# Two transfers of the norm's gain and bias: asked for earlier in layer A, as a repeating transfer into another buffer in layer B

## The chip, the cores and the metric

The kernel runs on one core of one Trainium2 chip. The metric is the device time of one launch in microseconds (us). Several executions are timed and their median is quoted; one more execution is profiled, and every start, duration and wait in this text is of that one.

## The reference

A decoder trunk of two layers over 256 tokens of width 1024, all float32. Layer A mixes the tokens with a gated linear recurrence (6 heads), layer B with stick-breaking attention (12 heads); both also attend to 256 memory tokens with 4 heads. Each layer ends in an output projection with a residual and a layer norm, and a mixture of 16 experts (2 per token) with a second residual and norm. What matters here, cut to its core:

```python
def post_norm(x, y, g, b):
    return layer_norm(DEEPNORM_ALPHA * x + y.astype(x.dtype), g, b)
...
        mixed = jnp.concatenate([seq_out.astype(x.dtype), mem_out.astype(x.dtype)], axis=-1)
        x = post_norm(x, mixed @ w_o[layer], ln_mix_g[layer], ln_mix_b[layer])
        moe_out = hier_moe(x, w_group[layer], b_group[layer], w_router[layer], b_router[layer],
                           w_gate[layer], w_up[layer], w_down[layer])
        x = post_norm(x, moe_out, ln_ffn_g[layer], ln_ffn_b[layer])
```

## The kernel before, in words

All weights are one array of 133 chunks, w0 to w132, each a tile of 128 partitions by 8 KB (1.05 MB). The class Stream sends them from SP's queue in the order of use. A chunk needs a free tile: from a ring of nine (tag w), or from a buffer that is idle just then and is lent to the stream by `stream.open(tags, end)` until chunk `end`. In the code no chunk is sent before the third one ahead of it has landed (DEPTH, L95 to L98), so at most three are in flight. A scheduler of the framework may exchange neighbours, but within an engine's queue the built order is fixed, and SP waits in that order.

The layer's second half is `mixer_end` (L937). For layer B (l = 1) it runs so. The last output projections give four sums of 128 tokens by 512. DVE adds the residual (L399, `Norm.add`). For the first half of the tokens ACT sums the squares (L406), DVE forms the variance (L409), POOL raises it to the power -0.5 (L410), and DVE continues with the shift (L413) and the ranking of that half's experts (`Moe.rank`, L580 to L597), in program order. Behind that stands the residual add of the last quarter of the tokens (L399 again), which PE needs for its transposes (L566), these for the second half's router logits (L573), then come the second half's statistics, its power (L424), ranking, slot counting (L604, L605) and the gather by a matrix of ones and zeros (L644). Then the experts begin: `Moe.run` works through eight pairs p = 0 to 7. Pair p of layer B uses chunks w85+6p to w90+6p: four for gate and up (L820; the first two in its first half, the next two in its second), two for down (L913). The first two products of pair p+1 are put between the gate and down products of pair p. w85 and w86 are sent on their own into tiles u and ex (L1574, L1575). Before the experts' end all engines read a count of tokens (`values_load`, L488); on SP that is one instruction, TENSOR_LOAD, that waits for a value from DVE, and chunks behind it wait with it.

The norm's gain and bias (two rows of 1024) must stand on all 128 partitions for the affine step (L438, L440: multiply and add, once for each half of the tokens). `rows` (L376) brings them into the tile gb: either ACT asks for 8 KB into one partition (L382) and POOL copies them to all partitions with two PARTITION_BROADCAST (L384), or, with `by_transfer`, one transfer writes the two rows to each of the 128 partitions (L380; 1.05 MB). Before, both layers' first norm use the former; the last norm of layer B uses the latter. POOL's broadcast belongs to a set of instructions of its own: the program loads it ahead (MODIFY_POOL_CONFIG at L384) and loads the other set back ahead of the next power (MODIFY_POOL_CONFIG at L410).

Around layer B's norm, buffers go to the stream like this: x0 and x1 (the projections' input, split in two) after the last projection (L1553); u, ex after the heads; m0, m1 and others in `mixer_end`; gb (which held the values vB until the last head product) only after the second affine step (L1078), until chunk 121.

Of the kernel before, what the change touches and what calls it, by code (L numbers as in the profile page):

```python
# [7 lines left out]
F32 = mybir.dt.float32  # L8
# [7 lines left out]
P = 128  # L16
D = 1024
T = 256
NT = 2
# [11 lines left out]
EXPERTS_END = (71, 133)  # L31
# [11 lines left out]
def trunk(ctx: ExitStack, tc: tile.TileContext, w_all, x_tok_d, cst_d, msk_d, rw_d, rb_d,  # L43
# [4 lines left out]
    slots = ctx.enter_context(tc.tile_pool(name="slots", bufs=1))  # L48
    keep = ctx.enter_context(tc.tile_pool(name="keep", bufs=1))
# [65 lines left out]
    def run(*gens):  # L115
        for g in gens:
            for _ in g:
                pass

    def chain(*gens):  # L120
        for g in gens:
            yield from g
# [10 lines left out]
    stream = Stream()  # L133
# [107 lines left out]
    def proj_feat(xs, evac, name, pre=None):  # L241

        w, i = pre[0] if pre else stream.get()
        xh, xl = xs
        ps = bank(f"{name}p", shape=(P, 2, T))
        for b in range(2):
            wh, wl = pre[1][b] if pre else split(w[:, b * HC:(b + 1) * HC], f"{name}{b}")
            for k in range(NK):
                s = slice(k * P, (k + 1) * P)
                nc.tensor.matmul(ps[:, b], wh[:, s], xh[:, k], start=(k == 0), stop=False)  # L250
                nc.tensor.matmul(ps[:, b], wh[:, s], xl[:, k], start=False, stop=False)
                nc.tensor.matmul(ps[:, b], wl[:, s], xh[:, k], start=False, stop=(k == NK - 1))
            if b == 0:
                yield
        stream.done(i)
        evac(ps)
        yield
# [8 lines left out]
    def proj_tok(xs, width, evac, name):  # L266

        c0 = 0
        while c0 < width:
            n = 512 if width - c0 >= 512 else 256  # L270
            kc = HC // n
            ps = [bank(f"{name}p{c0}_{t}", shape=(P, n)) for t in range(NT)]
            for k0 in range(0, NK, kc):
                hf = k0 // kc % 2
                if hf == 0:
                    w, i = stream.get()
                wh, wl = split(w[:, hf * HC:(hf + 1) * HC], f"{name}{c0}_{k0}")
                for k in range(kc):
                    for t in range(NT):
                        tok_mm(ps[t], xs, t, k0 + k, wh[:, k * n:(k + 1) * n], wl[:, k * n:(k + 1) * n],  # L280
                               k0 + k == NK - 1)
                if hf == 1:
                    stream.done(i)
                if k0 + kc < NK:
                    yield
            for t in range(NT):
                evac(t, c0, n, ps[t])
            yield
            c0 += n
# [22 lines left out]
    def mem_v(ms, l):  # L312
        return proj_tok(ms, 256, lambda t, c0, n, ps: nc.scalar.activation(memv[:, t], ps, AF.Copy), f"mv{l}")
# [59 lines left out]
    def tok_tile(which, name):  # L373
        return keep.tile([P, NT, D], F32, tag=which, name=name)

    def rows(which, name, by_transfer=False):  # L376

        gb = tok_tile("gb", f"gb{name}")
        if by_transfer:
            nc.scalar.dma_start(gb, ln_d[0, 2 * which:2 * which + 2].partition_broadcast(P))  # L380
            return gb
        nc.scalar.dma_start(gb[0:1], ln_d[:, 2 * which:2 * which + 2])  # L382
        for v in range(2):
            ins = nc.gpsimd.partition_broadcast(gb[:, v], gb[0:1, v])  # L384
            if which % 2:
                tc.keep_in_program_order(ins)
        return gb
# [44 lines left out]
    def affine(dst, z, gb, norms=None, ts=range(NT)):  # L432

        for t in ts:
            if norms:
                ins = nc.vector.scalar_tensor_tensor(dst[:, t], z[:, t], norms[t].r, gb[:, 0], op0=ALU.mult, op1=ALU.mult)
            else:
                ins = nc.vector.tensor_mul(dst[:, t], z[:, t], gb[:, 0])  # L438
            tc.keep_in_program_order(ins)
            tc.keep_in_program_order(nc.vector.tensor_add(dst[:, t], dst[:, t], gb[:, 1]))  # L440
# [493 lines left out]
            self.y = y  # L934


    def mixer_end(op, res, l, lasts, fill, finish):  # L937

        tags[0] = "m"
        s = res  # L940
        end = EXPERTS_END[l]
# [8 lines left out]
        norms = [Norm(f"x{l}{t}") for t in range(NT)]  # L950
# [117 lines left out]
        moe.start(work)  # L1068
        moe.indices()
        xg = moe.first_rows()  # L1070
        gb = rows(2 * l, f"m{l}")
        for p in moe.run(xg):
            if p == 0:
                x1 = moe.x1 = tok_tile("u", f"x1{l}")
                affine(x1, s, gb, ts=(0,))
            if p is None:
                affine(x1, s, gb, ts=(1,))
                stream.open(("gb",), end - 12, keep)  # L1078
            if p == 6 + l:
                gb = rows(2 * l + 1, f"o{l}", l == 1)  # L1080
        tags[0] = "my"
        z2 = tok_tile("v", f"z{l}")
        norms = [Norm(f"m{l}{t}") for t in range(NT)]
# [30 lines left out]
    with tc.tile_pool(name="lev", bufs=1) as lev:  # L1114
        q, kk, f = [slots.tile([P, NK, T], F32, tag=tag, name=name)[:, 0:NH]
                    for tag, name in (("o0", "q"), ("o1", "kk"), ("wc", "f"))]
# [125 lines left out]
        def ev_v(t, c0, n, ps):  # L1242
# [3 lines left out]
        fl = chain(proj_tok(xs, 768, ev_v, "ai"),  # L1246
                   proj_feat(xs, lambda ps: nc.scalar.activation(qm, ps, AF.Copy), "aqm"),
                   mem_k(ms, 0, load_split), mem_v(ms, 0))
# [7 lines left out]
    with tc.tile_pool(name="atta", bufs=1, reuse_waits="tile") as pool:  # L1256
        fl = proj_tok(xs, 768, ev_g, "ag")
# [14 lines left out]
    op = OutProj(mixed, 0, gn)  # L1272
    tags[0] = "m"
    op.start()
    with tc.tile_pool(name="hatt", bufs=1, reuse_waits="tile") as ha:
        def head(hg, t):
            po = bank("ho", shape=(P, 2, P))
            for j in range(2):
                h = 2 * hg + j
                hv = slice(h * P, (h + 1) * P)  # L1280
                if t == 0:
                    nc.tensor.matmul(po[:, j], AT[:, h, 0], v[:, 0, hv], start=True, stop=True)
                else:
                    nc.tensor.matmul(po[:, j], ATx[h // 3][:, h % 3], v[:, 0, hv], start=True, stop=False)
                    nc.tensor.matmul(po[:, j], AT[:, h, 1], v[:, 1, hv], start=False, stop=True)
            sq = ha.tile([P, 2, P], F32, tag="sq", name="sq", bufs=2)
            nc.scalar.activation(sq, po, AF.Square)  # L1287
            rms = ha.tile([P, 2], F32, tag="rms", name="rms", bufs=2)
            nc.vector.reduce_sum(rms, sq, axis=AX.X)
            nc.vector.tensor_scalar(rms, rms, 1.0 / P, RMS_EPS, op0=ALU.mult, op1=ALU.add)  # L1290
            nc.gpsimd.tensor_tensor(rms, rms, neghalf.to_broadcast([P, 2]), op=ALU.pow)  # L1291
            on = ha.tile([P, 2, P], F32, tag="on", name="on", bufs=2)
            nc.vector.tensor_mul(on, po, rms[:, :, None].to_broadcast([P, 2, P]))
            nc.vector.tensor_mul(on, on, gate[:, t].rearrange("p (h e) -> p h e", e=P)[:, 2 * hg:2 * hg + 2])
            return on

        def head_mixed(hg, t, on):
            pt = bank("hot", shape=(P, 2, P))
            for j in range(2):
                nc.tensor.transpose(pt[:, j], on[:, j], ident)  # L1300
            ks, ts_ = slice(2 * hg, 2 * hg + 2), slice(t * P, (t + 1) * P)
            nc.scalar.activation(mixed[0][:, ks, ts_], pt, AF.Copy)
            nc.vector.tensor_sub(mixed[1][:, ks, ts_], pt, mixed[0][:, ks, ts_])

        def heads():
            prev = None
            for hg in range(3):
                for t in range(NT):
                    on = head(hg, t)
                    if prev:  # L1310
                        head_mixed(*prev)
                    prev = hg, t, on
                    yield
            head_mixed(*prev)
            yield
        fl = op.main(range(3))
        weave(heads(), fl, 1)
        run(fl)
    x_tok = tok_tile("v", "x_tok")
    nc.scalar.dma_start(x_tok, x_tok_d)  # L1320
    stream.send(EXPERTS_END[0] - 48, keep, "u")
# [20 lines left out]
    fl = mem_v_fill()  # L1342
# [5 lines left out]
    def into_next(moe, work, add, norms, s, sc, gb):  # L1348
# [102 lines left out]
        stream.done(wk.chunk[1])  # L1451
        wparts.use(*free)
        wparts.turn = 2
    x2, gb, norms = mixer_end(op, x_tok, 0, [3], fl, into_next)


    mixed = fpair("o", "mixB")
    with tc.tile_pool(name="sbp", bufs=1, reuse_waits="tile") as sbp:
# [84 lines left out]
        fl = proj_tok(xs, 768, ev_v, "bv")  # L1543
        weave(sticks(range(4, 8)), chain(kq[2], qmp), 1.5)
        run(kq[2], qmp)
        with tc.tile_pool(name="attb", bufs=1, reuse_waits="tile") as pool:
# [3 lines left out]
            weave(chain(sticks(range(8, 12)), mem_attn(pool, qm, 1, prs, mixed, place)), fl, 6 / 14)  # L1550
            turned(11, betas.pop(11))
            run(fl)
    stream.open(("x0", "x1"), EXPERTS_END[1])  # L1553
    wparts.use("wa", "wb", "wc", "wd")
    op = OutProj(mixed, 1)
    tags[0] = "m"
# [13 lines left out]
    fl = op.main(range(2))  # L1570
    next(fl)
    weave(heads(), fl, 0.5)
    run(fl)
    stream.send(EXPERTS_END[1] - 48, keep, "u")  # L1574
    stream.send(EXPERTS_END[1] - 47, slots, "ex")  # L1575
    for q in (2, 3):
# [4 lines left out]
    def into_output(moe, work, add, norms, s, o, gb):  # L1581
# [10 lines left out]
        with tc.manual_schedule(engines={mybir.EngineType.DVE}):  # L1592
# [15 lines left out]
            gain(1, 1)  # L1608
            bias(1, 0)
            bias(1, 1)  # L1610
    mixer_end(op, x2, 1, [2, 3], iter(()), into_output)


# [88 lines left out]
```

## Time and profile before

| | us |
|---|---|
| median of 3 executions | 525.6 |
| lowest and highest | 524.14, 529.12 |
| the profiled execution's own time | 526.96 |
| its span (first to last instruction) | 525.3 |
| outside of the span | 1.66 |

PE is busy for 491.1 us of the span (93%), DVE for 300.2, ACT for 229.6, POOL for 62.9. The DMA engines moved 161.61 MB, 308 GB/s on average. The mean granted TensorE clock is 0.983.

The profile shows starts and durations on each engine, what ended the idle time before an instruction, and, by stretch, the share of the 16 DMA engines in use. An instruction that DMA issues is given without its landing; a landing shows indirectly, where the issue of a later chunk waits for it.

### The profile page before, as it was taken

The numbers are of one execution on the slowest core, as the hardware profiler recorded it, in microseconds if no ns is written. First come the engines' busy times: TensorE is split into PE (matmuls) and PEld (weight loads), VectorE is DVE, ScalarE is ACT, GpSimd is POOL, SyncE is SP. The second block draws the span as 40 slices with busy tenths as digits, with TensorE's granted clock in tenths as the row PEclk, the third lists the DMA queues.
The fourth block names the chain that finished last, engine by engine and source line by source line (L and its number), as shares of the span: only waits on it lengthen the run. The fifth ranks groups of instructions, "written<-read, shape, count | busy, mean of one in ns | idle before, by whom it ended". The sixth has DMA issues, their size and how long they took to land. (4 is left out here: it accounts for less than half of the span.)

```text
span 525.3 us, 9096 instructions
## 1 busy us (share of the span) xinstructions
PE 491.1 (93%) x3534; PEld 326.7 (62%) x3534; DVE 300.2 (57%) x682; ACT 229.6 (44%) x471; POOL 62.9 (12%) x78
## 2 busy tenths in 40 slices
PE   4999999999999999999797999998998899999992
PEld 4998898788996333333236889877687333333431
DVE  4668876867758622233338698677445842233547
ACT  4845446684445222333017566668423232222322
POOL 1100000002132111112011500000010121111201
PEclk9999999999999999999898999999998999999997
DMA  8999834447888999999999763242999799999922
GB/s 270 407 404 404 345 103 160 161 156 326 299 332 321 384 403 384 394 385 407 409 379 395 271 252 143 100 160 99 381 365 364 288 382 419 414 422 409 412 119 81
DMA packets 28439, 161.61 MB, mean 308 GB/s; under 512 B 5239, under 2 KB 5623, under 8 KB 11363
## 3 DMA queue, kind: packets, MB, share of 16 engines
q1 hardware_dynamic: 20736, 140.76, 68.3%
q0 software_dynamic: 4752, 10.94, 5.4%
q10 hardware_dynamic: 2902, 9.26, 4.8%
q8 instruction: 30, 0.49, 0.4%
q14 instruction: 19, 0.16, 0.1%
HBM read 158.92 MB, written 13.64 MB: 329 GB/s over the span
## 5 line engine op out<-in xcount | busy, mean ns | idle before, releaser
L820 PE MATMUL gu<-w,ex 128*64 128x512 f32 x256 | 62.9, 609 | 3.4 <-DMA w<-in_w_all_dram 2.3
L820 PE MATMUL gu<-w,xg 128*64 128x512 f32 x256 | 60.8, 601 | 0.1
L913 PE MATMUL po<-w,hT 128*64 128x512 f32 (+1 forms) x272 | 58.4, 570 | 0.1
L913 PEld LDWEIGHTS po<-w,hT 128*64 128x64 f32 x272 | 18.8, 136 | 34.0 <-issue 27.3
L820 PEld LDWEIGHTS gu<-w,ex 128*64 128x64 f32 x256 | 17.2, 137 | 34.8 <-issue 26.1
L820 PEld LDWEIGHTS gu<-w,xg 128*64 128x64 f32 x256 | 16.4, 136 | 26.5 <-issue 24.6
L920 DVE COPY hr<-po 128x512 f32<-128x512 f32 x10 | 6.9, 692 | 43.1 <-PE po L913 43.0
L629 ACT ACTIVATE xg<-xgp,lnT 128x128 f32<-128x128 f32 x32 | 13.5, 457 | 25.6 <-PE xgp L791 22.4
L918 DVE TENSOR_TENSOR hl<-po,hl 128x512 fp32r<-128x512 f32 (+1 forms) x14 | 8.5, 615 | 26.5 <-ACT hl L917 25.5
L627 DVE TENSOR_SCALAR xg<-xgp,lnT 128x128 f32<-128x128 f32 x32 | 12.4, 408 | 19.0 <-ACT xg L629 15.7
L629 ACT ACTIVATE ex<-xgp,lnT 128x128 f32<-128x128 f32 x32 | 14.3, 458 | 19.3 <-PE xgp L791 19.0
L627 DVE TENSOR_SCALAR ex<-xgp,lnT 128x128 f32<-128x128 f32 x32 | 13.1, 410 | 15.1 <-ACT ex L629 13.9
L900 ACT ACTIVATE hT<-ht 128x256 f32<-128x256 f32 (+1 forms) x18 | 6.5, 360 | 34.4 <-PE ht L899 34.3
L873 ACT ACTIVATE h<-gu 128x256 f32<-128x256 f32 (+1 forms) x18 | 6.3, 360 | 34.3 <-PE gu L820 34.3
L234 DVE TENSOR_TENSOR wo<-w,wo 128x512 fp32r<-128x512 f32 x20 | 13.7, 727 | 10.8 <-ACT wo L226 10.8
L760 POOL DMA_INDIRECT hd<-hr,own x10 | 10.1, 1014 | 81.2 <-DVE gsl L780 76.3
L673 POOL DMA_INDIRECT zg<-zd,idx x14 | 14.6, 1041 | 43.2 <-PE xgp L791 25.1
L791 PEld LDWEIGHTS xgp<-cst,zg 128*128 128x128 f32 x112 | 12.0, 141 | 11.4 <-PE gu L820 7.3
L1291 POOL TENSOR_TENSOR rms<-rms,neghalf 128x2 f32<-128x2 f32 x6 | 4.1, 699 | 111.6 <-ACT sq L1287 99.4
L384 POOL PARTITION_BROADCAST gbm<-gbm x4 | 5.3, 1398 | 94.2 <-DMA gbm<-in_ln_dram 85.5
L226 ACT ACTIVATE wo<-w 128x512 fp32r<-128x512 f32 x20 | 11.5, 628 | 9.8 <-PE wo L472 8.2
L917 ACT ACTIVATE hl<-po 128x512 fp32r<-128x512 f32 (+1 forms) x14 | 7.5, 537 | 18.4 <-PE po L913 18.4
(462 smaller groups left out, 1357.7 us busy)
## 6 DMA issues: line engine op xcount, KB each, us to landing
w<-in_w_all_dram SPq DMA_DIRECT2D x131, 1024.0 KB
hd<-in_w_all_dram ACTq DMA_DIRECT2D x2, 2560.0 KB
w<-in_w_all_dram SPq DMA_DIRECT2D x6, 256.0 KB
x_tok<-in_x_tok_dram ACTq DMA_DIRECT2D x1, 1024.0 KB
zd<-z ACTq DMA_DIRECT2D x2, 512.0 KB
gbo<-in_ln_dram ACTq DMA_DIRECT2D x1, 1024.0 KB
out_dram<-z SPq DMA_DIRECT2D x4, 256.0 KB
w<-in_w_all_dram SPq DMA_DIRECT2D x1, 512.0 KB
```

Of the source, the lines that this page charges most:

```text
L226: self.last_hi = nc.scalar.activation(p[:, 0, s], src[:, s], AF.Copy, scale=1.0 if scale is None else scale).ins
L234: nc.vector.tensor_sub(p[:, 1, s], src[:, s], p[:, 0, s])
L627: ins = nc.vector.tensor_scalar(xg[:, kk], ps, g, b, op0=ALU.mult, op1=ALU.add)
L629: nc.scalar.activation(xg[:, kk], ps, AF.Identity, scale=g, bias=b)
L673: nc.gpsimd.indirect_dma_start(out=self.zg[:, p % 2], out_offset=None, in_=self.zd, in_offset=bass.IndirectOffsetOnAxis(ap=self.idx[:, p:p ...
L760: pin(nc.gpsimd.indirect_dma_start(out=self.hd, out_offset=bass.IndirectOffsetOnAxis(ap=self.own[:, p:p + 1], axis=0), in_=src, in_offset= ...
L791: pin(nc.tensor.transpose(ps[:, k], self.zg[:, p % 2, (4 * hk + k) * P:(4 * hk + k + 1) * P], ident))
L820: pin(nc.tensor.matmul(gus[p][c * 64:(c + 1) * 64], xgs[p][:, kk, c * CAP:(c + 1) * CAP], ws[p][2 * kh + c][0][:, k * 512:(k + 1) * 512], ...
L913: pin(nc.tensor.matmul(po[c * 64:(c + 1) * 64], hT[:, f, c * 64:(c + 1) * 64], ws[p][4 + c][0][:, f * D + s.start:f * D + s.stop], start=( ...
L917: self.hl_last = nc.scalar.activation(hl[:, 0, s], po, AF.Copy).ins
L918: pin(nc.vector.tensor_sub(hl[:, 1, s], po, hl[:, 0, s]))
L920: nc.vector.tensor_copy(hr[:, p % 2, s], po)
```

## The change

In layer A the request for gain and bias is written ahead of the request for the residual tokens x_tok (before: behind the first expert rows). In layer B the rows come by the repeating transfer, into a tile with the tag x1 that is taken as soon as the projections' input is dead. So x1 goes to the stream later (after the second affine step, until the last chunk) and gb earlier (after the heads, until chunk 121).

```diff
-    def rows(which, name, by_transfer=False):
-
-        gb = tok_tile("gb", f"gb{name}")
+    def rows(which, name, by_transfer=False, gb=None):
+
+        gb = tok_tile("gb", f"gb{name}") if gb is None else gb
...
-    def mixer_end(op, res, l, lasts, fill, finish):
+    def mixer_end(op, res, gb, l, lasts, fill, finish):
...
-        gb = rows(2 * l, f"m{l}")
...
-                stream.open(("gb",), end - 12, keep)
+                stream.open(*((("gb",), end - 12, keep), (("x1",), end))[l])
...
+    gb = rows(0, "m0")
     x_tok = tok_tile("v", "x_tok")
...
-    stream.open(("x0", "x1"), EXPERTS_END[1])
+    gb1 = rows(2, "m1", True, slots.tile([P, NT, D], F32, tag="x1", name="gbm1"))
+    stream.open(("x0",), EXPERTS_END[1])
...
     run(fl)
+    stream.open(("gb",), EXPERTS_END[1] - 12, keep)
     stream.send(EXPERTS_END[1] - 48, keep, "u")
```

In the built programs layer A is the same: on all five engines its instructions stand in the same order, and with the same kinds of waits. ACT asks for x_tok first and for gain and bias two rows later, before as after. Up to the end of layer B's projections nothing moves on any engine.

On POOL, ahead of layer B's norm, before (normx is the norm's small tile, gbm holds gain and bias, the two ISA rows are the loads of the instruction sets):

```order
L1476 COPY diag<-cst 128x128 x2
L384 ISA
L384 ISA gbm_4341<-gbm_4341 128x1024 x2
L410 ISA
L410 TENSOR_TENSOR normx_4103<-normx_4103,neghalf 128x1
L424 TENSOR_TENSOR normx_4104<-normx_4104,neghalf 128x1
```

The same place now:

```order
L1474 MEMSET Q_3166 128x1
L1476 COPY diag<-cst 128x128 x2
L410 TENSOR_TENSOR normx_4105<-normx_4105,neghalf 128x1
L424 TENSOR_TENSOR normx_4106<-normx_4106,neghalf 128x1
L673 DMA zg_4305<-zd_4104,idx_4306 128x1024 x3
```

The two broadcasts and both loads of an instruction set are gone between the last copy and the first power.

On SP, at the start of layer B's experts, before (the number behind w is the chunk's):

```order
L94 DMA w101_4148<-in_w_all_dram 128x2048
L94 DMA w100_4146<-in_w_all_dram 128x2048
L94 DMA w104_4244<-in_w_all_dram 128x2048
L94 DMA w103_4242<-in_w_all_dram 128x2048
L488 TENSOR_LOAD most1_4378
L488 ISA x2
L94 DMA w102_4240<-in_w_all_dram 128x2048
L94 DMA w105_4394<-in_w_all_dram 128x2048
L94 DMA w106_4396<-in_w_all_dram 128x2048
L94 DMA w107_4414<-in_w_all_dram 128x2048
```

The same place now:

```order
L94 DMA w99_4088<-in_w_all_dram 128x2048
L94 DMA w100_4148<-in_w_all_dram 128x2048
L94 DMA w104_4246<-in_w_all_dram 128x2048
L488 TENSOR_LOAD most1_4376
L488 ISA x2
L94 DMA w103_4244<-in_w_all_dram 128x2048
L94 DMA w102_4242<-in_w_all_dram 128x2048
L94 DMA w107_4412<-in_w_all_dram 128x2048
L94 DMA w105_4392<-in_w_all_dram 128x2048
L94 DMA w106_4394<-in_w_all_dram 128x2048
```

w103 now stands behind the read of the count, and w107, whose tile is x1 and waits for the second affine step, stands ahead of w105 and w106 instead of behind them. Farther up SP's queue w95 goes into gb: it stood fourth of the group that starts with w92, and now stands behind w86, waiting for the last head product as w85 behind it does. On ACT the request for gain and bias moves from behind the last head's evictions to right behind the last eviction of vB.

## Rows read from the trace of the kernel before

**Rows 1.** Stages: busy us of each engine, granted clock, DMA share, GB/s.
```profile
360.00:370.00 10.00, 10.00 (x81) 7.79 (x81) 6.35 (x12) 7.35 (x17) 0.00 (x0) 1.00 0.60 227
370.00:380.00 10.00, 10.00 (x58) 6.97 (x56) 3.77 (x7) 3.99 (x9) 0.00 (x0) 1.00 0.98 391
...
403.00:405.00 2.00, 2.00 (x11) 2.00 (x11) 0.90 (x6) 0.00 (x0) 0.00 (x0) 0.50 0.85 250
...
411.00:416.00 5.00, 5.00 (x26) 1.60 (x24) 4.17 (x15) 0.10 (x1) 2.24 (x2) 1.00 0.65 212
416.00:420.00 4.00, 3.13 (x16) 0.87 (x12) 2.67 (x7) 1.00 (x4) 0.00 (x0) 1.00 1.02 411
...
430.00:490.00 60.00, 60.00 (x301) 21.26 (x298) 17.52 (x47) 15.29 (x35) 10.10 (x10) 1.00 1.02 415
```

**Rows 2.** SP's queue in order of time (start, duration): issues of expert chunks, layer B.
```profile
402.46 0.33 SPq L94 DMA_DIRECT2D w<-in_w_all_dram  x1
...
411.74 0.33 SPq L94 DMA_DIRECT2D w<-in_w_all_dram  x1
...
420.80 0.33 SPq L94 DMA_DIRECT2D w<-in_w_all_dram  x1
...
428.67 0.33 SPq L94 DMA_DIRECT2D w<-in_w_all_dram  x1
...
492.20 0.33 SPq L94 DMA_DIRECT2D w<-in_w_all_dram  x1
```

**Rows 3.** PE in order of time, the last pair of experts.
```profile
493.06 1.89 PE L820 MATMUL gu<-w,ex 128*64 128x512 f32 x8
...
501.85 4.46 PE L820 MATMUL gu<-w,ex 128*64 128x512 f32 x20
```

**Rows 4.** Waits of SP's queue, 400 to 412 (total, times, longest).
```profile
SPq L488 <- DVE gs L705: 8.5, 1, 8.5
```

**Rows 5.** DVE in order of time, layer B's norm and second affine step.
```profile
394.66 0.15 DVE L409 TENSOR_SCALAR normx<-normx 128x1 f32<-128x1 f32 x1 [1.32 <-ACT P L406]
...
398.83 0.68 DVE L399 SCALAR_TENSOR_TENSOR z<-z,wo 128x512 f32<-128x512 f32 x1
...
400.52 0.15 DVE L423 TENSOR_SCALAR normx<-normx 128x1 f32<-128x1 f32 x1
...
419.52 1.22 DVE L440 TENSOR_TENSOR x<-x,gbm 128x1024 f32<-128x1024 f32 x1
```

**Rows 6.** POOL in order of time, 375 to 425 (in brackets: idle before, releaser).
```profile
383.01 2.48 POOL L384 PARTITION_BROADCAST gbm<-gbm  x2 [85.50 <-DMA gbm<-in_ln_dram]
396.10 0.59 POOL L410 TENSOR_TENSOR normx<-normx,neghalf 128x1 f32<-128x1 f32 x1 [10.61 <-issue]
400.76 0.56 POOL L424 TENSOR_TENSOR normx<-normx,neghalf 128x1 f32<-128x1 f32 x1 [4.07 <-DVE pos L608]
```

**Rows 7.** Line 410: loads of POOL's instruction set, first and last start.
```profile
L410 POOLq MODIFY_POOL_CONFIG  x6: 127/127/127, 147.7 to 385.4; - x6
```

**Rows 8.** DVE in layer A: the first half's variance.
```profile
153.10 0.14 DVE L409 TENSOR_SCALAR normx<-normx 128x1 f32<-128x1 f32 x1
```

**Rows 9.** POOL in layer A: the first half's power.
```profile
155.87 0.59 POOL L410 TENSOR_TENSOR normx<-normx,neghalf 128x1 f32<-128x1 f32 x1 [8.07 <-issue]
```

**Rows 10.** PE in order of time, from the last output projection to the gather.
```profile
397.29 0.39 PE L472 MATMUL wo<-wo,mixB 128*128 128x512 f32 x1
397.52 0.96 PE L573 MATMUL lg<-rw,sT 128*128 128x20 f32 x8
398.97 0.18 PE L605 MATMUL slot<-Ab,trib 128*128 128x16 bf16 x1 [0.48 <-DVE Ab L597]
399.57 0.66 PE L566 MATMUL zt<-cst,z 128*128 128x128 f32 x4 [0.42 <-DVE z L399]
...
401.95 3.54 PE L644 MATMUL xgp<-P,z 128*128 128x128 f32 x16
...
406.24 2.02 PE L644 MATMUL xgp<-P,z 128*128 128x128 f32 x16 [0.71 <-DVE dl L690]
```

More of the change, by code (lines that the diff above doesn't have):

```diff
@@ L1453, in into_next @@
         wparts.turn = 2
-    x2, gb, norms = mixer_end(op, x_tok, 0, [3], fl, into_next)
+    x2, gb, norms = mixer_end(op, x_tok, gb, 0, [3], fl, into_next)
     mixed = fpair("o", "mixB")
@@ L1610, in into_output @@
             bias(1, 1)
-    mixer_end(op, x2, 1, [2, 3], iter(()), into_output)
+    mixer_end(op, x2, gb1, 1, [2, 3], iter(()), into_output)
 _INS = ["w_all", "x_tok", "cst", "msk", "rw", "rb", "lnT", "ln", "lowT"]
```

## The prediction

> **What bounds the kernel now.** I read the page first, then the stages by window, then the waits of SP, then each engine in order of time around layer B's norm. The reader is to see three things.
>
> First, layer B's expert stage is full twice over. From 430 to 490 PE is busy for all of 60.00 us, and the DMA engines' share is 1.02 at 415 GB/s [rows 1]. PE does not wait, but it does not lead by much either. A chunk's landing is seen where a later issue waits for it: w131 waits for w128, and it is issued at 492.20 [rows 2]. PE starts the products of w127 and w128 at 493.06, and every second one of the eight takes w128, so w128 is first needed 1.89 / 8 = 0.24 us later, at 493.30 [rows 3]. The slack of w128 is 493.30 - 492.20 = 1.1 us. The chunks behind it have more: w129 to w132 are all first used after 501.85 [rows 3].
>
> Second, the stream loses time just before. SP reads the count behind the issue of 402.46 and waits 8.5 us for it; the next chunk goes out at 411.74 [rows 2, 4]. From 411 to 416 the DMA share is 0.65, so 5 x 0.35 = 1.75 us stand empty; from 416 on it is 1.02 at 411 GB/s [rows 1].
>
> Third, the power of the first half of the tokens starts late on POOL. Its input is there at 394.66 + 0.15 = 394.81 [rows 5], it starts at 396.10 [rows 6]. The second power starts at 400.76, after an input that ends at 400.52 + 0.15 = 400.67, so a handover takes 0.09 [rows 5, 6]. The first could have started at 394.90 and is 1.2 us late. The profile names no other engine for this wait ("issue"), and the instruction set that the broadcast displaced began to load at 385.4 [rows 7]. I take the load for the cause.
>
> **Layer A.** The request is written earlier, but nothing in the built order moves, so I cost it at 0. The same late power is there: input at 153.10 + 0.14 = 153.24 [rows 8], start at 155.87 [rows 9], 2.6 us late, and that stays.
>
> **Layer B, what is removed.** Two broadcasts (2.48 us of POOL time [rows 6]) and both loads of an instruction set. POOL is idle around them, so their own time is worth nothing; what counts is the late power. With it 1.2 us earlier the shift and the ranking on DVE are 1.2 us earlier, and the residual add behind them could start at 398.83 - 1.2 = 397.63 [rows 5]. But its sum is ready only when the last output product ends, 397.29 + 0.39 = 397.68 [rows 10]. So it starts at about 397.7 and ends 1.1 us earlier. PE ends the logits at 397.52 + 0.96 = 398.48, does the slot product (0.18) without its wait of 0.48, and begins the transposes at 398.66 instead of 399.57 [rows 10]: 0.9 us earlier. From there to the first expert product each step waits for the one before it, PE, ACT and DVE in turn, so the lead of 0.9 us is handed on: to the count, to the second affine step, and to the experts.
>
> **Layer B, what is added.** One transfer of 1.05 MB instead of 8 KB. It is asked for by ACT at about 367, right after the projections' last eviction. ACT issues one DMA before and after, at a place where it is busy for 7.35 of 10 us and PE for all 10 [rows 1]; cover enough for an issue, and I cost it at 0. Gain and bias are needed at the first affine step, over 40 us later, so that wait is free too. The bytes are not: the DMA share is 0.60 from 360 to 370 but 0.98 from 370 to 380 [rows 1]. The new transfer takes the place that w95 had, whose tile is now gb, free only after the last head product. So from there on the stream is one chunk behind, and that is why w103 stands behind the read of the count.
>
> **What is moved on SP.** Before, from 411.74: w102, two gathers of 0.52 MB, then w105, w106, and at 420.80, 0.06 us after the second affine step ended (419.52 + 1.22 = 420.74), w107 [rows 2, 5]. All four have landed when w110 is issued at 428.67, since w110 waits for w107 [rows 2]. Now the count is read at 411.74 - 0.9 = 410.84 and w103 and w102 follow. With the empty 1.75 us the data begin at 412.6; two chunks and two gathers are 3.15 MB, at 411 GB/s 7.7 us: 420.3. SP meanwhile stands at w107, whose tile x1 is read until 420.74 - 0.9 = 419.84, and w105 and w106, whose tiles are free by then, queue behind it. Issued at 419.9, with 1.75 us to the first data: 421.6. Between 420.3 and 421.6 the DMA engines have next to nothing to move. Three chunks and half of the next gather are 3.41 MB, 8.3 us: 429.9.
>
> The same arithmetic for before gives 411.74 + 1.75 + 5.1 (w102 and the gathers) + 8.3 = 426.9, and the marker shows 428.67. Against the arithmetic the stream is 429.9 - 426.9 = 3.0 us late, against the marker 1.2. The difference is handover and a rate that was not full, and I do not know how much of it stays. I take the middle, 2.1 us. Bounds: if w103 finds its place wholly in time that was empty, the stream is not late at all and leads by 0.9; if it costs a full transfer (1.05 / 0.411 = 2.55 us) and a full new gap (1.4), without any lead, it is 3.95 late. From 430 on the DMA engines are full, so what is late stays late. The last norm's own transfer into gb comes one pair of experts later than before, since gb now serves w114; it still lies ahead of w128, so it takes as much from the stream as before.
>
> **The sum.** w128 lands 2.1 us later with 1.1 us of slack: the end moves by 2.1 - 1.1 = +1.0 us. PE's lead of 0.9 us turns into a longer wait for w128. The profiled execution would take 526.96 + 1.0 = 527.96. Its own time is 1.36 above the median of the runs shown, so against that median I predict 525.6 + 1.0 = 526.6. With the bounds the end moves by -0.9 (lead kept, no wait) to 3.95 - 1.1 = +2.85: 524.7 to 528.45.
>
> **Rivals.**
> - The fall of the clock goes too. From 403 to 405 the granted clock is 0.50, its lower level (1.2 instead of 2.4 GHz) [rows 1]; the gather's first 16 passes take 3.54 us there, the other 16 take 2.02. Ahead of it PE had waited 0.48 and 0.42 us [rows 10]. Both waits shrink, which speaks for it; the wait for ACT behind the transposes stays, which speaks against. Price: 1.5 us more lead, so the count and the affine step are 1.5 earlier, the stream is 0.6 late, and the end moves by 0.6 - 1.1 = -0.5: 525.1. In "TensorE: Matmul & The Clock Gate", Part 1, the Trainium skill lets the gate follow how busy PE has just been, and the rows agree with that.
> - No lead. The power waits for something else than the load. The load that began at 385.4 would have to take 10.7 us to hold it up [rows 6, 7], and in layer A the one that began at 147.7 only 8.2 [rows 7, 9], which speaks against the load; that both powers are late speaks for it. Without the lead all of SP's steps are 0.9 later, the stream is 3.0 late, the end moves by +1.9: 527.5. The Trainium skill's "GPSIMD Engine Reference", section 2.1 (Instruction dispatch), gives about 6 us for the code load at the first call of a freshly loaded kernel; by that figure it would end at 391.4, before the input is there, and this rival would hold. The rows show longer ones.
> - Starvation, the slower side: not one chunk but two are late. w95 waits for the last head product at the front of SP's queue, with w85 and all others behind it; if the DMA engines run empty there as they do before the count, that is a second transfer. Price: 2 x 2.55 + 1.4 - 0.9 = 5.6 us late, the end at 5.6 - 1.1 = +4.5: 530.1. It decides from the point at which w128 lands more than 3.95 us later. Against it: before, w85 waited for the same product, and the share there was 0.98 [rows 1].
> - The change does more than the order shows: layer A's set is loaded in time after all, and its 2.6 us go [rows 8, 9]. The end moves by up to 1.0 - 2.6 = -1.6: 524.0. Nothing in the order speaks for it.
>
> **How the numbers follow.** Forecast 0.72, clock 0.14, no lead 0.04, starvation 0.07, layer A 0.03. About 1% (5.3 us) is what a measurement of this kernel can tell from no change, and the three runs shown lie 5 us apart. None of the cases reaches -1%; a low median alone could, 0.04. Slower by over 1% needs starvation or a high median: 0.08. Within 1%: 0.88. The range starts from the cases (524.0 to 530.1, most of the chance between 524.7 and 528.45) with the spread of a median of a few runs on top: 523.8 to 529.4.
>
> **What would show it.** Right: in layer B the power starts within 0.2 us of its input; PE begins the second half's transposes about 0.9 us earlier against the last output product; SP issues one chunk fewer ahead of the count; a gap in the DMA share just ahead of w107; then a new PE wait for a chunk, of about 2 us, in the first products of the last pair, and no other. Layer A keeps its late power. Wrong: no wait of PE for w128 (then the stream has caught up, and the end is earlier by the lead), a power that is still late, or waits for chunks in several pairs.

## The result, and the profile after

| | before | after |
|---|---|---|
| median, us (20 executions each) | 525.92 | 528.53 |
| lowest and highest, us | 519.08, 530.39 | 522.70, 533.08 |
| ratio of the times, with its 95% interval | | 1.0063 [1.0039, 1.0087] |
| span of the profiled execution, us | 525.3 | 528.6 |
| mean granted TensorE clock | 0.983 | 0.986 |

The changed kernel is slower by 0.63%: 0.0063 x 525.9 = 3.3 us, by the interval 2.1 to 4.6. The ratio compares the fast executions of both kernels alone, so it is not the quotient of the two medians, which lie 2.6 us apart. The prediction had said +1.0, so the sign is right, the median lies in the range, and the forecast is a third of what came.

The profile is read in the order of the prediction's steps. Layer A on DVE and POOL (start, duration, in brackets the idle time before and what ended it), to be held against [rows 8, 9]:

```profile
154.55 0.14 DVE L409 TENSOR_SCALAR normx<-normx 128x1 f32<-128x1 f32 x1
```
```profile
157.47 0.59 POOL L410 TENSOR_TENSOR normx<-normx,neghalf 128x1 f32<-128x1 f32 x1 [8.01 <-issue]
```

The power still starts 157.47 - 154.69 = 2.8 us after its input. Nothing has moved in layer A.

Layer B's norm on DVE, POOL and PE, to be held against [rows 5, 6, 10]:

```profile
391.87 0.15 DVE L409 TENSOR_SCALAR normx<-normx 128x1 f32<-128x1 f32 x1 [1.32 <-ACT P L406]
...
414.00 1.23 DVE L440 TENSOR_TENSOR x<-x,gbm 128x1024 f32<-128x1024 f32 x1
```
```profile
392.11 0.55 POOL L410 TENSOR_TENSOR normx<-normx,neghalf 128x1 f32<-128x1 f32 x1 [97.36 <-DVE normx L409]
```
```profile
394.50 0.39 PE L472 MATMUL wo<-wo,mixB 128*128 128x512 f32 x1
394.74 0.96 PE L573 MATMUL lg<-rw,sT 128*128 128x20 f32 x8
395.55 0.17 PE L605 MATMUL slot<-Ab,trib 128*128 128x16 bf16 x1
395.69 0.66 PE L566 MATMUL zt<-cst,z 128*128 128x128 f32 x4
...
397.94 2.03 PE L644 MATMUL xgp<-P,z 128*128 128x128 f32 x16
...
400.72 2.02 PE L644 MATMUL xgp<-P,z 128*128 128x128 f32 x16 [0.71 <-DVE dl L690]
```

The power now starts 392.11 - 392.02 = 0.09 us after its input and names DVE as its releaser. The slot product has lost its wait. The transposes start 395.69 - 394.89 = 0.80 after the last output product; before it was 399.57 - 397.68 = 1.89. Both gathers take 2.0 us, so the clock did not fall here in this execution.

SP's queue around the count (its waits from 400 to 440: total, times, longest; then issues in order of time), to be held against [rows 2, 4]:

```profile
SPq L488 <- DVE gs L705: 9.3, 1, 9.3
SPq L94 <- DVE x L440: 7.5, 1, 7.5
```
```profile
406.18 0.33 SPq L94 DMA_DIRECT2D w<-in_w_all_dram  x1
...
415.25 1.34 SPq L94 DMA_DIRECT2D w<-in_w_all_dram  x3
423.20 0.83 SPq L94 DMA_DIRECT2D w<-in_w_all_dram  x2
427.16 0.33 SPq L94 DMA_DIRECT2D w<-in_w_all_dram  x1
431.32 0.33 SPq L94 DMA_DIRECT2D w<-in_w_all_dram  x1
436.36 0.80 SPq L94 DMA_DIRECT2D w<-in_w_all_dram  x2
...
493.69 0.33 SPq L94 DMA_DIRECT2D w<-in_w_all_dram  x1
```

SP stands at w107 until 415.25, right behind the second affine step (414.00 + 1.23 = 415.23), with w105 and w106 behind it. Then the chunks come in bursts: two at 423, single ones at 427 and 431, nothing for 5.0 us, two at 436. In the built order there is a second exchange that the prediction did not quote: w110 stands ahead of w109. So w112, which waits for w109, cannot go out before 436.36, and w113 follows at once.

The stages (busy us of each engine, granted clock, DMA share, GB/s), to be held against [rows 1]:

```profile
415.00:418.00 3.00, 2.31 (x14) 1.34 (x16) 1.26 (x4) 2.15 (x5) 0.97 (x1) 1.00 0.73 279
...
430.00:436.00 6.00, 6.00 (x34) 2.32 (x30) 0.92 (x3) 0.69 (x2) 1.01 (x1) 1.00 1.02 421
...
436.00:439.00 3.00, 3.00 (x17) 1.06 (x17) 1.64 (x4) 1.69 (x4) 1.02 (x1) 1.00 0.88 287
448.00:451.00 3.00, 3.00 (x17) 1.22 (x17) 1.64 (x4) 1.79 (x4) 1.04 (x2) 1.00 0.96 336
460.00:463.00 3.00, 3.00 (x20) 1.41 (x20) 1.76 (x5) 1.79 (x4) 1.37 (x2) 1.00 0.99 377
472.00:475.00 3.00, 3.00 (x20) 1.54 (x20) 1.51 (x4) 1.79 (x4) 0.64 (x1) 1.00 0.87 352
...
430.00:485.00 55.00, 54.88 (x274) 19.30 (x271) 15.67 (x38) 14.47 (x32) 9.32 (x10) 1.00 0.99 392
...
492.90:499.70 6.80, 6.03 (x12) 2.37 (x12) 2.45 (x2) 0.00 (x0) 0.00 (x0) 0.50 1.01 421
```

The first row is the gap ahead of w107. The rows from 436 on are a pattern that nobody had forecast: every 12 us, once in a pair of experts, the transfers thin out. From 430 to 485 the DMA engines move 392 GB/s; in the trace of the kernel before the same stretch reads:

```profile
430.00:485.00 55.00, 55.00 (x272) 19.35 (x270) 15.91 (x43) 13.82 (x32) 7.10 (x7) 1.00 1.02 416
```

At 392 instead of 416 GB/s, 55 us bring 55 x 24 / 416 = 3.2 us less of transfer. The last pair pays for it (PE in order of time, against [rows 3]):

```profile
490.94 1.04 PE L820 MATMUL gu<-w,ex 128*64 128x512 f32 x2 [2.12 <-DMA w<-in_w_all_dram]
493.67 3.68 PE L820 MATMUL gu<-w,ex 128*64 128x512 f32 x6 [1.69 <-DMA w<-in_w_all_dram]
...
512.59 3.66 PE L913 MATMUL po<-w,hT 128*64 128x512 f32 x24
```

PE waits 2.12 us for w127 and 1.69 for w128; before, it waited for no chunk in this layer. From 492.9 on, within the second wait, the granted clock stands at 0.50 for 6.8 us, its lower level, and six products take 3.68 us instead of 6 x 1.89 / 8 = 1.42.

**Where the time went.** The two executions are compared from one event, the end of the first half's variance (394.81 before, 392.02 after), because they were already 2.79 us apart there, in code that is the same. (In layer A, PE waits for a chunk in both: 2.30 us at 254.79 before, 1.04 at 253.86 after; the clock then fell to 0.51 for 3.4 us before, and again at 282.2, and neither time after.) The marks are the first expert product and the last down products, before:

```profile
409.44 3.65 PE L820 MATMUL gu<-w,xg 128*64 128x512 f32 x16
...
509.13 3.66 PE L913 MATMUL po<-w,hT 128*64 128x512 f32 x24
```

and the first expert product after:

```profile
403.92 3.65 PE L820 MATMUL gu<-w,xg 128*64 128x512 f32 x16
```

From the variance to the first expert product it was 14.63 and is 11.90: 2.73 less, of which 1.5 is the clock that did not fall during the gather. From there to the start of the last down products it was 99.69 and is 108.67: 9.0 more, made of PE's waits for w127 and w128 (3.8), a wait for a gather in pair 0 (0.8), and the low clock (PE is busy 6.03 us at half speed, so 3.0 lost); 1.4 is left unassigned. Together +6.3, less the 2.8 from ahead: +3.5, and the spans say +3.3. The ratio of the times says +3.3 as well, but it rests on many executions, and the thirteen profiles of this text show that the clock falls differ from one to the next, so the agreement is partly luck.

### The profile page after: what moved, and what is told of

Same layout as the page of the kernel before. It is cut to its first block, busy times and chain, and to the rows that moved or that the text cites. A ratio compares the mean times of both kernels' runs of the same rounds, so it can differ in the third digit from the quotient of the medians.

```text
span 528.6 us, 9087 instructions
## 1 busy us (share of the span) xinstructions
PE 491.8 (93%) x3534; PEld 326.0 (62%) x3534; DVE 300.8 (57%) x682; ACT 229.7 (43%) x471; POOL 61.3 (12%) x76
## 5 line engine op out<-in xcount | busy, mean ns | idle before, releaser
L820 PE MATMUL gu<-w,ex 128*64 128x512 f32 x256 | 64.1, 610 | 4.8 <-DMA w<-in_w_all_dram 4.8
L820 PE MATMUL gu<-w,xg 128*64 128x512 f32 x256 | 60.8, 601 | 0.1
L820 PEld LDWEIGHTS gu<-w,ex 128*64 128x64 f32 x256 | 17.5, 138 | 37.3 <-issue 29.5
L820 PEld LDWEIGHTS gu<-w,xg 128*64 128x64 f32 x256 | 16.4, 136 | 26.5 <-issue 24.6
L791 PEld LDWEIGHTS xgp<-cst,zg 128*128 128x128 f32 x112 | 12.0, 141 | 12.2 <-PE gu L820 7.3
L791 PE MATMUL xgp<-cst,zg 128*128 128x128 f32 x112 | 15.3, 279 | 0.8 <-DMA zg<-zd,idx 0.8
L922 ACT ACTIVATE hr<-po 128x512 f32<-128x512 f32 x10 | 6.0, 597 | 21.8 <-PE po L913 21.8
```

What stands on the lines that cost most here:

```text
L791: pin(nc.tensor.transpose(ps[:, k], self.zg[:, p % 2, (4 * hk + k) * P:(4 * hk + k + 1) * P], ident))
L820: pin(nc.tensor.matmul(gus[p][c * 64:(c + 1) * 64], xgs[p][:, kk, c * CAP:(c + 1) * CAP], ws[p][2 * kh + c][0][:, k * 512:(k + 1) * 512], ...
```

## The experiments

Three theories were held against each other. **Stream**: the chunks come too late for the last pair. **Exchange**: it is the exchange of tiles, gain and bias into x1 and a chunk's wait for x1, that costs. **Clock**: the fall of the clock is the loss. Two quantities serve in all runs. The first is PE's wait for chunks in the last pair. The second is the distance from the first expert product to the issue that waits for w128 (the marker of [rows 2]). It is 492.20 - 409.44 = 82.8 before and 493.69 - 403.92 = 89.8 after. When nothing waits, w128 is first used 84.1 behind the first product: the pieces x2 and x6 of the last pair show that the third of the eight products is the first to take it, so before this was at 493.06 + 2 x 1.89 / 8 = 493.53. (The prediction had let every second product take it, and said 493.30.) Other short waits of PE in between can move that date by some tenths.

| | ratio to before | PE's wait for chunks | distance | GB/s, 430 to 485 |
|---|---|---|---|---|
| before | 1 | 0 | 82.8 | 416 |
| after | 1.0063 [1.0039, 1.0087] | 3.8 | 89.8 | 392 |
| e1 transfer, old tile | 1.0062 [1.0026, 1.0099] | 2.9 | 88.1 | 405 |
| e7 the same, chunks in order | 0.9941 [0.9896, 0.9986] | 0 | 82.5 | 415 |
| e3 after, chunks in order | 0.9982 [0.9946, 1.0018] | 0 | 84.2 | 415 |
| e4 after, last norm by broadcast | 0.9980 [0.9946, 1.0015] | 1.0 | 85.9 | 397 |
| e8 e3 and e4 together | 0.9974 [0.9936, 1.0012] | 0 | 82.8 | 414 |
| e2 broadcast into the new tile | 0.9985 [0.9949, 1.0022] | 1.6 | 86.4 | 404 |
| e5 e2 and e4 together | 1.0005 [0.9959, 1.0051] | 0 | 79.4 | 415 |
| e6 e5, layer A by transfer | 0.9918 [0.9888, 0.9947] | 0 | 80.4 | 406 |
| e9 before, layer A by transfer | 0.9927 [0.9886, 0.9969] | 0 | 81.9 | 411 |
| e10 e7, layer A by transfer | 0.9912 [0.9880, 0.9944] | 0 | 82.8 | 409 |
| e11 e3, layer A by transfer | 0.9897 [0.9867, 0.9927] | 0 | 84.8 | 416 |

The last three columns are of one execution each. The layer B of e10 is that of e7, and the layer B of e6 that of e5, yet their rates differ by 6 and 9 GB/s, so differences of that size say little. And the clock fell during the gather in before and e5 to e10, which delays PE there, and not in after, e1 to e4 and e11; after and e3 are alike in this, e1 and e7 are not. The ratios do not have this weakness.

**e1, the transfer without the exchange of tiles** (against before):

```diff
-        gb = rows(2 * l, f"m{l}")
+        gb = rows(2 * l, f"m{l}", l == 1)
```

> Only the repeating transfer, in the tile gb and at the old place; x0 and x1 go to the stream as before. In the built order w107 again stands ahead of w105 and w106, and w110 ahead of w109. Theory S (the chunk stream is late: one transfer more, and chunks out of order): 3 us above the kernel before, like the change, with PE waits for a chunk in the last pair of experts. Rival X (what costs is the exchange of x1 and gb): no more than 0.5 us from the kernel before, or below it by the power's lead of 1 us.

Measured: 1.0062, as slow as the change. PE, last pair:

```profile
486.60 1.04 PE L820 MATMUL gu<-w,ex 128*64 128x512 f32 x2 [0.49 <-DMA w<-in_w_all_dram]
490.09 3.18 PE L820 MATMUL gu<-w,ex 128*64 128x512 f32 x6 [2.44 <-DMA w<-in_w_all_dram]
```

Waits at the same products, and slow products behind: from 490.6 on the granted clock is 0.51 for 3.4 us. The exchange of tiles is not needed for the loss. But here too the scheduler had put w107 ahead of w105 and w106, and w110 ahead of w109, and four more pairs of neighbours behind them were exchanged. So bytes and order were still mixed.

**e2, the new tile without the transfer** (against after):

```diff
-    gb1 = rows(2, "m1", True, slots.tile([P, NT, D], F32, tag="x1", name="gbm1"))
+    gb1 = rows(2, "m1", False, slots.tile([P, NT, D], F32, tag="x1", name="gbm1"))
```

> The change, but gain and bias of layer B come by the 8 KB request and POOL's broadcast, into x1, early. No transfer of 1.05 MB; chunks w105 to w113 in order; the instruction set can be loaded back long before the power. Theory S: no PE wait for a chunk in the last pair beyond 1 us, the power starts on time, time 0.5 to 2 us below the kernel before. Rival X: 2 to 3 us above it.

Measured: 0.9985, no difference from before that can be told; one wait, longer than the 1 us that was expected, and no clock fall behind it:

```profile
489.50 1.93 PE L820 MATMUL gu<-w,ex 128*64 128x512 f32 x6 [1.60 <-DMA w<-in_w_all_dram]
```

The chunks stand in the order of the program here. The power is on time although POOL broadcasts: the broadcast starts at 365.27, 26 us ahead of the power (at 391.35) in place of 13 [rows 6], and the load of the other set begins at 368.0. That takes the exchange of tiles off the list: with it, and without the bytes and the exchanged chunks, no loss is seen. Why this kernel moves only 404 GB/s with its chunks in order stays open.

**e3, the change with the order of the chunks held** (against after; from w105 on):

```diff
+            if i > 84 + 48 - 28:
+                tc.keep_in_program_order(ins)
```

> The change with SP's chunks from w105 on held in the program's order (w105, w106, w107, w108, w109, w110); nothing else moves. Theory S with the order as the larger part: the gap ahead of w107 and the thin flight before w112 go, and 1.5 to 2.5 us of the change's 3.3 us with them (0.8 to 1.8 us above the kernel before). If the transfer's bytes are the whole cost: 3 us above it, as the change.

Measured: 0.9982; the loss is gone, with the same bytes and the same tiles, and all of it, where 1.5 to 2.5 us had been expected. Stages and PE:

```profile
436.00:439.00 3.00, 3.00 (x16) 0.86 (x12) 0.00 (x0) 0.60 (x1) 0.00 (x0) 1.00 1.02 418
448.00:451.00 3.00, 3.00 (x18) 0.87 (x14) 0.00 (x0) 0.60 (x1) 0.00 (x0) 1.00 1.03 427
...
430.00:485.00 55.00, 55.00 (x270) 19.35 (x270) 17.04 (x45) 14.99 (x35) 8.13 (x8) 1.00 1.01 415
```
```profile
495.25 1.89 PE L822 MATMUL gu<-w,ex 128*64 128x512 f32 x8
```

The thin spots are gone, the rate is back at 415 GB/s, and the eight products run in one piece. (Two lines of this kernel are added, so L820 reads L822.) On PE, ACT and POOL the instructions stand in the same order in both traces. The hold undoes both exchanges at once, w107 ahead of w105 and w110 ahead of w109; no run parts them.

This profiled execution took 529.43 us, 3.6 above the kernel's median, and lost its time in layer A, whose code is that of before. The power there is 161.51 - 153.42 = 8.1 us late:

```profile
153.28 0.14 DVE L411 TENSOR_SCALAR normx<-normx 128x1 f32<-128x1 f32 x1
```
```profile
161.51 0.59 POOL L412 TENSOR_TENSOR normx<-normx,neghalf 128x1 f32<-128x1 f32 x1 [12.09 <-issue]
```

**e4, the change with the last norm's rows by broadcast** (against after):

```diff
-                gb = rows(2 * l + 1, f"o{l}", l == 1)
+                gb = rows(2 * l + 1, f"o{l}")
```

> The change, with the last norm's gain and bias by 8 KB and POOL's broadcast instead of the 1.05 MB transfer that runs while the last chunks come. Theory S: w127 and w128 land 2.5 us earlier, their PE waits shrink from 3.8 us to 1.5 or less, time 2 to 3 us below the change. Rival C (the difference is the TensorE clock, not the stream): as the change, 3.3 us above the kernel before.

Measured: 0.9980, 4.4 us below the change, where 2 to 3 had been expected. This kernel has the exchanged order of the change and its thin spots (397 GB/s), but 1.05 MB less to move ahead of w128. The wait shrinks to one of 1.0 us, with no clock fall behind it:

```profile
490.16 1.93 PE L820 MATMUL gu<-w,ex 128*64 128x512 f32 x6 [1.01 <-DMA w<-in_w_all_dram]
```

So the loss can be paid for on either side: fewer bytes, or no thin spots. That is what a stream that is late against a fixed date does, and what neither the exchange nor a clock that falls by itself would do.

**e5, neither large transfer in layer B; e6, and layer A by one** (e5: the edits of e2 and e4; e6 adds, against after):

```diff
-    gb = rows(0, "m0")
+    gb = rows(0, "m0", True)
```

> Both earlier edits together: gain and bias of layer B's first norm by POOL's broadcast into x1 (early), the last norm's by POOL's broadcast too; chunks in order, no transfer of 1.05 MB for a norm. Theory S: the stream is 2.5 us earlier at the last pair than with the first edit alone, so no PE wait for a chunk is left, and the time is 1 to 3 us below the kernel before. If the stream did not bound: the same as with the first edit alone, 0.8 us below the kernel before.

> As the kernel without large transfers, but layer A's first norm gets gain and bias by the repeating transfer of 1.05 MB, so that no instruction set is loaded ahead of layer A's power. The power there starts at once instead of 2.6 us late. If layer A's stream has room: 1 to 2.5 us below that kernel. If the transfer's bytes cost there what they cost in layer B: no gain, or up to 2 us above it.

Measured: e5 1.0005, with the stream 79.4 us behind the first product, 4.7 ahead of its date. No gain is seen, neither of being early nor of the power on time, but the interval reaches from 2.2 us below to 2.7 above, so neither theory is decided by it. e6: 0.9918, faster than both kernels, and 4.6 us below e5, where 1 to 2.5 had been expected. Layer A's power is on time there.

**e7, e1 with the order held; e8, e3 and e4 together** (edits as above):

> The repeating transfer in the tile gb at the old place, as in the first experiment, but with SP's chunks from w105 on in the program's order. Theory S with the order as the larger part: within 1 us of the kernel before, where the same without the order stood 3.3 us above it; no fall of the granted clock in the last pair. If the transfer's bytes were the cost: 3 us above the kernel before.

> The change with the chunks in order and the last norm by POOL's broadcast. If both edits act through w127 and w128 alone, the second adds little to the first once the wait is gone: 1 to 2 us below the kernel before, the same as each of them alone within 1 us. If the two are independent costs: 4 to 5 us below the kernel before.

Measured: e7 0.9941 against e1's 1.0062, two intervals that do not touch, for the same bytes and the same tiles. Rates of e1 and e7, and e7's last pair:

```profile
430.00:485.00 55.00, 55.00 (x278) 19.86 (x276) 17.00 (x42) 15.67 (x35) 10.09 (x10) 1.00 1.00 405
```
```profile
430.00:485.00 55.00, 55.00 (x276) 19.51 (x274) 15.63 (x38) 14.58 (x33) 9.89 (x10) 1.00 1.01 415
```
```profile
489.25 1.89 PE L822 MATMUL gu<-w,ex 128*64 128x512 f32 x8
```

In the two traces the instructions of all five engines stand in the same order but for the chunks' numbers on SP. This is the clearest pair: the order of the chunks alone is worth 1.2%, by the ends of the intervals 0.4 to 2.0%. The expectation for e7, within 1 us of the kernel before, was too cautious: it is 3.1 us faster. e8 0.9974: the two cures do not add up, since either one alone already brings w128 in time or nearly so.

**e9, layer A by transfer in the kernel before; e10 and e11, the same in e7 and e3**:

```diff
-        gb = rows(2 * l, f"m{l}")
+        gb = rows(2 * l, f"m{l}", l == 0)
```

> The kernel before, with one edit: layer A's first norm gets its gain and bias by the repeating transfer (1.05 MB) in place of POOL's broadcast. Layer B is as before. In the run with layer A by transfer, an extra 1.05 MB came where the DMA share ahead of layer A's norm was 0.85, and layer A's power started on time in place of 2.6 us late. If the gain of that run (ratio 0.992) is layer A's power alone: ratio 0.993 to 0.997 (-1.5 to -3.5 us), POOL's first power of layer A within 0.2 us of its input, and no new PE wait for a chunk in layer A. If the gain there came from layer B's edits in that run: ratio 0.999 to 1.001 here. If the extra bytes in layer A cost a wait as in layer B: ratio over 1.002 and PE waits for a chunk in layer A.

> The kernel before, with both layers' first norm by the repeating transfer into the old tile, and the chunks from w105 on held in the order of the program. The run with layer B alone so was at ratio 0.994. If layer A's late power is worth its 2.6 us beside that: ratio 0.987 to 0.990 (-5 to -7 us), and no PE wait for a chunk in either layer. If what layer A gains is taken back as a longer PE wait for w127 or w128 in layer B: ratio 0.993 to 0.995, with such a wait of 1 us or more.

> The changed kernel with the chunks from w105 on held in the order of the program (0.998 in its own run) and layer A's first norm by the repeating transfer. If the order of the chunks was the loss and layer A's late power the gain that was not taken: ratio 0.991 to 0.994 (-3 to -5 us), PE waits for w of 1 us or less, layer A's power on time. If the stream of this kernel is at its limit even in order, PE's lead from layer A turns into a wait for w127 or w128: ratio 0.996 to 1.000, with a wait of 1 us or more and a clock fall behind it.

Measured: e9 0.9927 (0.993 to 0.997 expected for layer A's power alone), e10 0.9912, e11 0.9897. In e9, DVE, POOL and PE in layer A:

```profile
153.92 0.14 DVE L409 TENSOR_SCALAR normx<-normx 128x1 f32<-128x1 f32 x1
```
```profile
154.13 0.55 POOL L410 TENSOR_TENSOR normx<-normx,neghalf 128x1 f32<-128x1 f32 x1 [17.10 <-DVE normx L409]
```
```profile
166.30 3.65 PE L820 MATMUL gu<-w,xg 128*64 128x512 f32 x16
```

The same product before:

```profile
166.58 3.65 PE L820 MATMUL gu<-w,xg 128*64 128x512 f32 x16
```

The power follows its input by 0.07 us, and the first expert product follows it by 166.30 - 154.06 = 12.24, against 166.58 - 153.24 = 13.34 before: 1.1 us. The interval of e9 says 1.6 to 6.0 us, so this lead of one execution is not all of it. But the lateness differs between executions: in the nine profiles whose layer A is as before the power is 2.4 to 2.9 us late seven times, 3.9 in e5 and 8.1 in e3, and the first expert product stands on average 2.4 us farther behind the variance than in e9 (1.5 without e3). So the lead is worth more than the one execution shows; an estimate from nine executions leaves open whether it is all of the gain. In layer A too the chunks wait behind a read of the count that comes earlier with the power, and PE's wait for a chunk at the end of layer A (2.30 us before) is absent in the profiles of e6, e9, e10 and e11. That fits, but it is also absent in e1, e2, e5 and e7, and only 0.3 us long in e3, whose layer A is as before, so it is not shown. e10 missed its expectation (0.987 to 0.990): on top of e7 the transfer in layer A brings 0.3%, less than was expected but within the intervals, and the wait that the second theory asked for is not there. e11 did what the first theory said, and a little more (0.991 to 0.994 expected); w128 is still a little late in it, since the eight products take 2.33 us instead of 1.89. It is the change with two mends, and it is faster than both kernels: its interval lies below 1, and below that of the changed kernel.

## Why the prediction was right in sign and a third in size

- **Layer A, cost 0:** right. The power is 2.8 us late as before; the rival by which layer A moves falls.
- **The power of layer B:** right. It starts 0.09 us after its input. The load of the instruction set ahead of the power, 10.7 and 8.2 us from load to power [rows 6, 7, 9] and 12.2 in e3's layer A (149.33 to 161.51), was the cause: without it the power is on time in layer B, and in e9 in layer A, and so it is in e2, where the load stands 23.3 us ahead of the power. The rival without a lead falls. The Trainium skill's "GPSIMD Engine Reference", section 2.1 (Instruction dispatch), gives about 6 us for a code load at the first call of a freshly loaded kernel; the rows here are longer, and the measurement decides.
- **The lead:** 0.9 predicted at the transposes, 1.89 - 0.80 = 1.1 measured.
- **The clock at the gather:** this rival's mechanism came (0.50 before, 1.00 after, 1.5 us of lead), its outcome did not: the first expert product was 2.7 us earlier, and the end was later all the same. It is not shown to be a part of the change: of the other ten profiles with the power on time in layer B, five (e5 to e8 and e10) have a fall around 394 to 400 again.
- **SP's order, the gap ahead of w107, the lateness there:** right. In the time frame of before (2.79 added) the chunk behind the group w105 to w107 is issued at 427.16 + 2.79 = 429.95, against 428.67: 1.3 us late, where 1.2 to 3.0 had been worked out, and 0.6 for the case that came here, without a clock fall at the gather.
- **"From 430 on the DMA engines are full, so what is late stays late":** this step failed. The issue that waits for w128 comes at 493.69 + 2.79 = 496.48, against 492.20: 4.3 us late, 3.0 more than at w107, beyond the bound of 3.95. I had read the 1.02 share of before as a property of the stage. It depends on the order in which the chunks stand: with w110 ahead of w109 SP sends nothing for 5.0 us, the next two go out together, and the burst repeats in each pair, though PE's waits for the chunks show no further exchange in this kernel. After and e3, e4 and e8, e1 and e7 are three pairs with one and the other order: 392 and 415, 397 and 414, 405 and 415 GB/s. The order is not all, since e2 moves 404 with its chunks in order; and that it is w110, and not the gap ahead of w107, that starts the bursts is argued from the times of the issues and not shown by a run of its own.
- **The sign:** in part luck. The slack of w128 is 493.53 - 492.20 = 1.3 us and not 1.1 (its first use was misread, see above). Had the lateness stayed at 1.3 us, the end would hardly have moved in this execution. What moved it is 4.3 - 1.3 = 3.0 us of lateness beyond the slack and 3.0 us of low clock behind the waits, together 6.0 of the 6.3 us from the variance on; the sum had taken its +1.0 from the lateness at w107 alone.
- **The place of the price:** right. The first products of the last pair wait, and those of no other pair; 2 us predicted, 3.8 measured.
- **What a wait costs:** not priced. The sum let a wait cost its own length. The low clock that came with it added 3.0 us of PE time in the profiled execution.
- **Starvation, two chunks late:** it decided "from the point at which w128 lands more than 3.95 us later", and that point was passed. But its cause is not the one found: w95 ahead of w85 is in e3 and e11 too, and they lose nothing.

That the exchange happens at all is the framework scheduler's doing; which of its costs sets it was not tried.

## What to carry to other kernels

Where a queue admits each transfer by the landing of an earlier one, read the whole built order of that queue after a change, and not only the place of the edit: exchanged neighbours far from it turned an even stream into bursts and cost more than the megabyte that was added, for e7 moves that megabyte in order and is not slower. Before an even stream is counted on ("the DMA engines are full, so late stays late"), ask what keeps it even; and hold the order where it matters. And take the same cure where it costs less: layer A had the same late power with bytes to spare, and there the transfer gained 0.7%.

## What the runs showed of the hardware that was not expected

A wait of PE for a chunk can cost nearly twice its length. The rows: with 2.12 and 1.69 us in after the granted clock was 0.50 for 6.8 us, behind 0.49 and 2.44 in e1 it was 0.51 for 3.4, and behind 2.30 us in layer A of before it was this:

```profile
254.90:258.30 3.40, 3.40 (x7) 0.56 (x7) 2.01 (x2) 0.00 (x0) 0.00 (x0) 0.51 1.00 412
```

Behind single waits of 1.0 (e4) and 1.6 us (e2) in layer B it stayed at 1.00; the row is of e2, whose wait ended at 489.50:

```profile
490.00:495.00 5.00, 5.00 (x22) 2.25 (x20) 2.45 (x2) 0.45 (x2) 0.00 (x0) 1.00 1.02 420
```

The length of the wait does not decide alone. In layer A a wait of 2.02 us (e4, ended at 253.43) and one of 2.05 (e8, at 255.14) had no fall behind them, nor had one of 2.81 us for DVE in after (at 278.84), where before had one (2.82, at 281.42). The row is of e4:

```profile
253.50:258.00 4.50, 4.50 (x18) 1.86 (x19) 1.89 (x2) 0.38 (x1) 0.00 (x0) 1.00 1.01 419
```

So a lateness can cost its own length or nearly twice that, and what decides is not shown. In the two profiles with the loss, after and e1, the fall came with two waits close together; in after its 3.0 us are part of why +1 us became +3.

The load of POOL's instruction set does not always take the same time. In nine executions with the same layer A the power came 7.9 us (e4) to 12.2 us (e3) after the start of the load, and so 2.4 to 8.1 us after its input; without the load it was under 0.1 in e6, e9, e10 and e11.
